# When transfers make the weight sums of the down projection: 18 from the output projection on, 14 during up

## The chip, the cores and the metric

The kernel runs on one core of a Trainium2 chip. A core has TensorE for matmuls (PE in the profile; PEld is its loading of weights), VectorE (DVE), ScalarE (ACT), GpSimd (POOL) and SyncE (SP), which only issues transfers. Transfers run on 16 DMA engines that the queues of SP, ACT and POOL share. The metric is the device time of one execution in microseconds, taken as the median over several runs.

## The reference

One encoder block on 512 tokens of width 2048, all in float32: a mixer of gated-DeltaNet and RWKV-7 heads, a cross-attention into 256 memory tokens, and an MLP, each added to the residual stream.

```python
xn = _rmsnorm(h, norm_mix[l])
y = xn @ w_in[l]
mixed = jnp.concatenate([o_gdn, o_rwkv], axis=-1)     # from y, the two mixers
h = h + mixed @ w_out[l]                              # the output projection
h = h + _cross_attention(...)
hn = _rmsnorm(h, norm_mlp[l])
h = h + jnp.square(jax.nn.relu(hn @ mlp_w_up[l])) @ mlp_w_down[l]   # up, then down; hidden 8192
return _rmsnorm(h, norm_final)
```

## The kernel before

Every float32 matmul is made of three: both operands are split into a high part (a cast, on ACT, L130) and a low part (a subtraction, on DVE, L131), and high x high, high x low and low x high are added up in PSUM. So every weight tile of 128x1024 passes through a load by SP, a cast whi on ACT and a subtraction wlo on DVE before TensorE gets it.

Up and down use a scheme with seven products in place of eight (Strassen in Winograd's form). In up this works on groups: `strassen(p, ...)` for p = 0 to 31 makes 256 of the 8192 hidden columns from four weight blocks (`a11`, `a21`, `a22`, `a12`, loaded at L1432) and sums of them made by DVE (L1408). The seven products go to PSUM tiles x, y and z. ACT and DVE bring them to two tiles of SBUF, c1 and c2, which come from a pool of three buffers, tag `sl`. The group ends with a square of c1 and of c2 on ACT (L1548), and the results, with two differences that DVE makes (t and t4), are written to DRAM (`Cd`, cd in the profile) by four transfers from ACT's queue:

```python
nc.scalar.dma_start(Cd[p // 2][:, 2:4, h], v(c2))     # L1497
nc.scalar.dma_start(Cd[p // 2][:, 0:2, h], v(c1))     # L1498
nc.scalar.dma_start(Cd[p // 2][:, 4:6, h], v(t))      # L1499
nc.scalar.dma_start(Cd[p // 2][:, 6, h], t4)          # L1500
```

The next group begins, for ACT, with the copy of x to the next c1 (L1466), and then with that of y to the next c2 (L1472), whose buffer is the one that L1497 is read from. A scheduler puts the instructions of each engine in order and adds the waits; an instruction behind a waiting one on the same engine waits too.

Down reads the hidden values back and takes four quarters (c = 0 to 3) of the hidden dimension one after another. Two of its seven products need sums of weight blocks. There are 32 of them, 1 MB each: `SUMS[0][u]` and `SUMS[1][u]` for u = 0 to 15, tiles in DRAM named ws in the profile, of which u = 4c to 4c + 3 belong to quarter c, the four of `SUMS[0]` needed ahead of the four of `SUMS[1]`. No engine computes these sums: POOL issues one transfer that copies a block from `w_dn` to the tile (L1304, shape 16x16384), waits until it has landed, and issues a second that adds the other block to it on the way (L1305, 512x512). `background` does this for all 32 in a row, held in that order. It is called in the output projection once the first of its 16 row blocks is there; a POOL copy of one column (L1301) makes it wait for that block. The two transfers of one sum are in order; the next sum's copy is issued right behind the add.

Of the kernel before, what the change touches and what calls it, by code (L numbers as in the profile page):

```python
# [9 lines left out]
F32 = mybir.dt.float32  # L10
F32R = mybir.dt.float32r
AF = mybir.ActivationFunctionType
ALU = mybir.AluOpType
# [4 lines left out]
P = 128  # L18
# [55 lines left out]
def build(tc, I, out):  # L74
    nc = tc.nc
    V, S, GP, PE = nc.vector, nc.scalar, nc.gpsimd, nc.tensor
    es = ExitStack()

    pc = es.enter_context(tc.tile_pool(name="pc", bufs=1))
# [18 lines left out]
    def col(name, i=0):  # L98
        o, w = PRM[name]
        return prm[:, o + i:o + i + 1]  # L100
# [17 lines left out]
    def psb(nm, tag="mx", bufs=2):  # L118
        return tile_of(ps, [P, 512], F32, tag, nm, bufs)
# [8 lines left out]
    def split(src, hi, lo, gain=None):  # L128
        if gain is None:
            S.copy(hi, src)  # L130
            V.tensor_tensor(out=lo, in0=src, in1=hi.bitcast(F32), op=ALU.subtract)  # L131
        else:
            S.activation(hi, src, AF.Copy, scale=gain)
            V.scalar_tensor_tensor(out=lo, in0=src, scalar=gain, in1=hi.bitcast(F32),
                                   op0=ALU.mult, op1=ALU.subtract)
# [20 lines left out]
    def gemm(pt, wsrc, nk, hi, lo):  # L156
        for h in range(nk // 8):
            wh, wl = wload(wsrc[:, h * 1024:(h + 1) * 1024] if nk > 8 else wsrc)
            for kk in range(8):
                k = h * 8 + kk  # L160
                sl = slice(kk * P, (kk + 1) * P)
                mm(pt, wh[:, sl], hi[k], start=(k == 0), stop=False)
                mm(pt, wh[:, sl], lo[k], start=False, stop=False)
                mm(pt, wl[:, sl], hi[k], start=False, stop=(k == nk - 1))
# [172 lines left out]
    def act_tile(nm, dt=F32R):  # L337
        return tile_of(pa, [P, 512], dt, "act", nm, 32)
# [5 lines left out]
    SUMS = {i: [pd.tile([P, 2048], F32, name=f"ws{i}_{u}", tag=f"ws{i}_{u}") for u in range(16)] for i in (0, 1)}  # L344
# [884 lines left out]
    hres = [hq[n // 4][n % 2][:, n // 2 % 2, :] for n in range(16)]  # L1229
# [4 lines left out]
    def sl2(w=512):  # L1234
        cnt[0] += 1
        return ph.tile([P, 512], F32, tag="sl", name=f"sl{cnt[0]}", bufs=3)[:, 0:w]
# [18 lines left out]
    for n2 in range(8):  # L1255
        hi, lo = act_tile(f"vhi{n2}"), act_tile(f"vlo{n2}")
        for i in range(2):
            n = 2 * n2 + i
# [11 lines left out]
            u, t = rstd[:, M:2 * M], sl2(M)  # L1270
# [7 lines left out]
    for g in range(4):  # L1278
        for h in range(4):
            pts = [psb(f"vo{g}_{h}_{mt}", ("mm", "mg")[h % 2]) for mt in range(2)]  # L1280
            for q in range(2):
                wh, wl = wload(I["wo"][g, h][:, q * 1024:(q + 1) * 1024])
                for mt in range(2):
                    for e in range(2):
                        d = q * 2 + e
# [9 lines left out]
                nc.scalar.dma_start(VOd[g][:, h * 2 + mt, :], ev)  # L1295


    def background(h):

        d = pc.tile([P, 1], F32, name="began")  # L1300
        tc.keep_in_program_order(GP.tensor_copy(d, h[:, 0:1]))  # L1301
        for u in range(16):
            for i, b in ((0, 2), (1, 0)):
                tc.keep_in_program_order(GP.dma_start(SUMS[i][u], I["w_dn"][u, b]))  # L1304
                tc.keep_in_program_order(GP.dma_start(SUMS[i][u], I["w_dn"][u, 1], accum_op=ALU.add, max_dma_last_dim=2048))  # L1305

    def finish(n, acc):
        if n == 0:
            S.activation(acc, hres[n], AF.Square)
        else:  # L1310
            sq = sl2()
            S.activation(sq, hres[n], AF.Square)
            V.tensor_tensor(out=acc, in0=acc, in1=sq, op=ALU.add)
# [3 lines left out]
    for n in range(KD):  # L1317
        xr = sl2()
        nc.sync.dma_start(xr, I["xT"][:, n, :])
        pt = psb(f"op{n}", "mm", 2)  # L1320
        gemm(pt, I["w_out"][n], KD, oh, ol)
        V.tensor_tensor(out=hres[n], in0=pt, in1=xr, op=ALU.add)
        hi, lo = act_tile(f"hh{n}"), act_tile(f"hl{n}")
        split(hres[n], hi, lo, col("norm_xattn", n))
        hh_.append(hi)
        hl_.append(lo)
        finish(n, acc)
        if n == 0:
            background(hres[n])
    pcol = psb("pcol")  # L1330
    for t in range(4):
        mm(pcol[:, t:t + 1], acc[:, t * P:(t + 1) * P], ones[:, 0:1])
# [10 lines left out]
    for g in range(2):  # L1343
        pts = [psb(f"sc{g}_{t}", ("mm", "mm", "mg", "mg")[t]) for t in range(4)]
        for n2 in range(8):
# [7 lines left out]
            for i in range(2):  # L1353
                n = 2 * n2 + i
# [49 lines left out]
    def sub(o, a, b):  # L1404
        V.tensor_tensor(out=o, in0=a, in1=b, op=ALU.subtract)

    def add(o, a, b):
        V.tensor_tensor(out=o, in0=a, in1=b, op=ALU.add)  # L1408
# [17 lines left out]
    def raw(src, own=None):  # L1426
        i = nraw[0] % 7 if own is None else own
        nraw[0] += 1
        r = pw.tile([P, 1024], F32, tag="wraw", name=f"ua{nraw[0]}", bufs=NWR) if i % 2 else \
            pu.tile([P, 1024], F32, tag="wraw2", name=f"ub{nraw[0]}", bufs=4)  # L1430
        if src is not None:
            nc.sync.dma_start(r, src)  # L1432
        return r

    def block(pt, a, parts, start):
        cnt[0] += 1
        hi = pw.tile([P, 1024], F32R, tag="whi", name=f"whi{cnt[0]}", bufs=NWS)
        lo = pw.tile([P, 1024], F32R, tag="wlo", name=f"wlo{cnt[0]}", bufs=NWS)
        split(a, hi, lo)
        for k in range(8):  # L1440
            for x in parts[k]:
                PE.matmul(pt, hi[:, k * P:k * P + P], x, start=start, stop=False, skip_group_check=True)  # L1442
                start = False
        for k in range(8):
            PE.matmul(pt, lo[:, k * P:k * P + P], parts[k][0], start=False, stop=k == 7, skip_group_check=True)  # L1445

    def strassen(p, done, used):

        def product(i, pt, a, start=True):
            block(pt[:, HA], a, [(comb[i][k][:, HA], comb[i][k][:, HB]) for k in range(8)], start)
            if used:
                used(i)

        if p == 0:
            a11, a12, a22, a21 = (raw(I["w_up"][p, i], o) for i, o in ((0, 1), (3, 1), (2, 1), (1, 0)))
        else:
            a11, a21, a22, a12 = (raw(I["w_up"][p, i]) for i in range(4))  # L1460
        s1 = raw(None, 0 if p == 0 else None)
        x, y, z = (psb(f"up{n}{p}", t) for n, t in (("x", "mx"), ("y", "mg"), ("z", "mm")))
        c1, c2 = sl2(), sl2()

        product(B11, x, a11)
        S.copy(c1[:, HA], x[:, HA])  # L1466
        if p == 0:
            product(B21, z, a12)
            sub(c1[:, HA], c1[:, HA], z[:, HA])
        add(s1, a21, a22)  # L1470
        product(T1, y, s1)
        S.copy(c2[:, HB], y[:, HA])  # L1472
        add(s1, s1, a11)
        product(T2, x, s1, False)
        S.copy(c1[:, HB], x[:, HA])
        add(a21, a21, a11)
        if p > 0:
            product(B21, z, a12)
            sub(c1[:, HA], c1[:, HA], z[:, HA])
        add(a12, a12, s1)  # L1480
        product(T3, x, a21, False)
        add(c2[:, HB], c2[:, HB], x[:, HA])
        product(B22, y, a12, False)
        add(c1[:, HB], c1[:, HB], y[:, HA])
        done(c1, ALU.min)
        product(T4, x, a22, False)
        S.copy(c2[:, HA], x[:, HA])
        done(c2, ALU.max)
        t = pu.tile([P, T], F32, tag="tt", name=f"tt{p}", bufs=2)
        t4 = pu.tile([P, M], F32, tag="t4", name=f"t4_{p}", bufs=1)  # L1490
        sub(t[:, HA], c1[:, HB], c1[:, HA])
        sub(c1[:, HB], c1[:, HB], c2[:, HB])
        sub(t[:, HB], c1[:, HA], c1[:, HB])
        sub(t4, c2[:, HA], t[:, HB])
        h = slice(p % 2 * M, p % 2 * M + M)
        v = lambda a: a.rearrange("p (a b) -> p a b", b=M)
        nc.scalar.dma_start(Cd[p // 2][:, 2:4, h], v(c2))  # L1497
# [3 lines that stand above are left out]
# [44 lines left out]
    for p in range(32):  # L1545
        def square(c, op):
            V.scalar_tensor_tensor(out=c, in0=c, scalar=0.0, in1=rstd, op0=op, op1=ALU.mult)
            S.activation(c, c, AF.Square)  # L1548

        def used(i):  # L1550
            if p == 0 and i == T1:
                pt = psb("pss2", "scr", 1)
                mm(pt, ones, acc)
                rsq(rstd, pt, 1.0 / 2048, b_eps6)
            if p == 31 and i in (T1, T2, T3):
                for q in ((0,), (1, 2), (3,))[i - T1]:
                    piece_(0, 0, q)

        strassen(p, square, used)
# [224 lines left out]
```

## Time and profile before

| | |
|---|---|
| median of three runs | 3033.95 us |
| lowest and highest | 3027.75, 3034.09 us |
| the profiled execution | 3031.7 us, its span 3029.9 us |
| TensorE busy | 2977.6 us (98%), granted clock 0.995 on average |
| ACT, DVE, POOL busy | 1481.0, 2078.6, 266.2 us |
| POOL's transfers (queue q0) | 67.11 MB, 9.2% of the 16 DMA engines' span |
| output projection | from 1333 us on |
| up | about 1690 to 2343 us |

In the profile's rows, "out<-in" names what an instruction writes and reads, "[6.55 <-DMA cd<-sl]" is idle time of its engine just before it and what ended that. Times in order of time are microseconds from the span's start, then the duration. ACTq and SPq are transfers that these engines' queues issue.

### The profile page before, as it was taken

To read this page: it belongs to the slowest core of one execution; us is meant where nothing else is said; L and a number is where in the kernel's file an instruction comes from. 1 tells how busy PE (TensorE), PEld (TensorE's weight loads), DVE (VectorE), ACT (ScalarE), POOL (GpSimd) and SP (SyncE) were. 2 spreads that over 40 slices of the span, in tenths; PEclk is the share of its full clock that TensorE was granted. 3 is DMA by queue.
4 is the path that set the end of the run, shared out by engine and by line. 5 is a ranking of instruction groups with operands and counts; after the bars stand their busy time and mean duration, and the time that the engine had idled before them with its cause. 6 is when DMAs were issued, how large, how long until landed. Compare 5 with 4: busy or idle time off the path is not lost.

```text
span 3029.9 us, 56109 instructions
## 1 busy us (share of the span) xinstructions
PE 2977.6 (98%) x22912; PEld 2677.1 (88%) x22912; DVE 2078.6 (69%) x2925; ACT 1481.0 (49%) x2000; POOL 266.2 (9%) x612
## 2 busy tenths in 40 slices
PE   9999999999999999999999889999999999999998
PEld 7788878878877898878887889999999999999998
DVE  7666666676677646534337778888888786868676
ACT  6454555554556555543326544444444544444444
POOL 0302312213213000001111100000000000000000
PEclk9999999999999999999999999999999999999999
DMA  5322323322425487789999974544544877676754
GB/s 185 102 87 80 108 79 83 108 81 81 136 65 164 149 269 239 253 266 265 260 252 261 247 228 154 153 149 146 161 147 147 278 243 239 213 250 197 241 181 153
DMA packets 284625, 537.70 MB, mean 177 GB/s; under 512 B 95752, under 2 KB 148236, under 8 KB 283856
## 3 DMA queue, kind: packets, MB, share of 16 engines
q1 hardware_dynamic: 228816, 427.15, 45.6%
q0 software_dynamic: 17920, 67.11, 9.2%
q10 hardware_dynamic: 37632, 39.86, 3.8%
q8 instruction: 179, 2.93, 0.4%
q14 instruction: 78, 0.64, 0.1%
HBM read 473.86 MB, written 127.28 MB: 198 GB/s over the span
## 4 chain that ended last, share of the span: by engine, by line
PE 89%; DMA 4%; DVE 3%; ACT 2%; issue 1%; POOL 0%; SPq 0%; DVEq 0%; ACTq 0%; POOLq 0%
PE py L247 21%; PE upx L1442 7%; PE dx L1442 7%; PE op L122 6%; PE upy L1442 4%; PE upx L1445 4%; PE dx L1445 4%; PE dy L1442 3%; PE vo L122 3%; PE sc L122 3%; PE at L122 3%; PE vp L122 3%; PE kq L247 3%; PE kp L247 3%; PE upz L1442 2%; PE upy L1445 2%
## 5 line engine op out<-in xcount | busy, mean ns | idle before, releaser
L130 ACT CAST whi<-ub 128x1024 fp32r<-128x1024 f32 x259 | 271.0, 1048 | 288.3 <-PE dx L1442 69.8
L131 DVE TENSOR_TENSOR wlo<-ub,whi 128x1024 fp32r<-128x1024 f32 x259 | 316.1, 1222 | 98.0 <-ACT whi L130 97.8
L247 PE MATMUL py<-xhi,whi 128*128 128x512 f32 x928 | 371.6, 400 | 6.6 <-ACT xhi L247 6.6
L247 PE MATMUL py<-xhi,wlo 128*128 128x512 f32 x928 | 372.0, 401 | 0.0
L247 PE MATMUL py<-xlo,whi 128*128 128x512 f32 x928 | 371.3, 400 | 0.0
L247 DVE TENSOR_TENSOR wlo<-wraw,whi 128x1024 fp32r<-128x1024 f32 (+1 forms) x180 | 223.4, 1241 | 128.7 <-ACT whi L247 127.0
L130 ACT CAST whi<-ua 128x1024 fp32r<-128x1024 f32 x189 | 198.0, 1048 | 212.2 <-PE dx L1442 51.8
L247 ACT CAST whi<-wraw 128x1024 fp32r<-128x1024 f32 (+1 forms) x180 | 188.2, 1045 | 204.1 <-PE py L247 161.9
L1442 PE MATMUL upx<-cb,whi 128*128 128x256 f32 x2048 | 268.5, 284 | 4.3 <-ACT whi L130 4.3
L131 DVE TENSOR_TENSOR wlo<-ua,whi 128x1024 fp32r<-128x1024 f32 x189 | 230.6, 1221 | 60.7 <-ACT whi L130 58.6
L1442 PEld LDWEIGHTS upx<-cb,whi 128*128 128x128 f32 x2048 | 256.5, 193 | 4.9 <-ACT whi L130 4.7
L1442 PE MATMUL dx<-dh,whi 128*128 128x256 f32 x1024 | 252.0, 284 | 3.1 <-ACT whi L130 3.1
L1442 PE MATMUL dx<-dl,whi 128*128 128x256 f32 x1024 | 251.2, 283 | 0.0
L131 DVE TENSOR_TENSOR wlo<-wraw,whi 128x1024 fp32r<-128x1024 f32 x112 | 137.3, 1226 | 111.3 <-ACT whi L130 109.9
L247 PEld LDWEIGHTS py<-xhi,whi 128*128 128x128 f32 x928 | 175.0, 189 | 40.9 <-ACT xhi L247 6.6
L247 PEld LDWEIGHTS py<-xhi,wlo 128*128 128x128 f32 x928 | 175.0, 189 | 35.3 <-issue 1.0
L247 PEld LDWEIGHTS py<-xlo,whi 128*128 128x128 f32 x928 | 174.9, 188 | 35.1 <-DVE xlo L247 0.7
L1442 PEld LDWEIGHTS dx<-dh,whi 128*128 128x128 f32 x1024 | 196.5, 192 | 4.3 <-ACT whi L130 4.1
L1442 PEld LDWEIGHTS dx<-dl,whi 128*128 128x128 f32 x1024 | 196.5, 192 | 0.0
L130 ACT CAST whi<-wraw 128x1024 fp32r<-128x1024 f32 x112 | 117.8, 1051 | 151.7 <-PE op L122 68.9
L1445 PE MATMUL upx<-cb,wlo 128*128 128x256 f32 x1024 | 144.5, 284 | 0.0
L1445 PE MATMUL dx<-dh,wlo 128*128 128x256 f32 x1024 | 143.8, 283 | 0.1
(782 smaller groups left out, 6982.5 us busy)
## 6 DMA issues: line engine op xcount, KB each, us to landing
wraw<-in_w_in SPq DMA_DIRECT2D x116, 512.0 KB, 3.8
ub<-in_w_dn SPq DMA_DIRECT2D x88, 512.0 KB, 5.1
ua<-in_w_dn SPq DMA_DIRECT2D x72, 512.0 KB, 4.9
ub<-in_w_up SPq DMA_DIRECT2D x71, 512.0 KB, 4.4
ws<-in_w_dn POOLq DMA_DIRECT2D x32, 1024.0 KB, 10.8
ua<-in_w_up SPq DMA_DIRECT2D x57, 512.0 KB, 4.3
sl<-cd SPq DMA_DIRECT2D x104, 256.0 KB, 5.3
ub<-ws SPq DMA_DIRECT2D x40, 512.0 KB, 5.1
```

The costliest lines, as they stand in the source:

```text
L122: PE.matmul(o, l, r, start=start, stop=stop)
L130: S.copy(hi, src)
L131: V.tensor_tensor(out=lo, in0=src, in1=hi.bitcast(F32), op=ALU.subtract)
L247: f(*a, **k)
L1442: PE.matmul(pt, hi[:, k * P:k * P + P], x, start=start, stop=False, skip_group_check=True)
L1445: PE.matmul(pt, lo[:, k * P:k * P + P], parts[k][0], start=False, stop=k == 7, skip_group_check=True)
```

## The change

`background` gets a count. Its first call, at the same place, makes 18 sums. Each further call makes one: it stands in `strassen` behind odd groups from p = 3 on, as long as any sum is left, that is 14 times, the last at p = 29. There ACT copies one column of the finished c2 to a column of a small tile `ticks`, POOL copies that to `tock`, and so waits for it, and then issues the two transfers. The sums are made in the order in which down needs them: the four of `SUMS[0]` of a quarter, then the four of `SUMS[1]`. Lines behind the change move by 3 to 6.

```diff
-    def background(h):
-
-        d = pc.tile([P, 1], F32, name="began")
-        tc.keep_in_program_order(GP.tensor_copy(d, h[:, 0:1]))
-        for u in range(16):
-            for i, b in ((0, 2), (1, 0)):
-                tc.keep_in_program_order(GP.dma_start(SUMS[i][u], I["w_dn"][u, b]))
-                tc.keep_in_program_order(GP.dma_start(SUMS[i][u], I["w_dn"][u, 1], accum_op=ALU.add, max_dma_last_dim=2048))
+    ticks = pc.tile([P, 32], F32, name="ticks")
+    tock = pc.tile([P, 1], F32, name="tock")
+    wanted = [(i, c * 4 + u) for c in range(4) for i in (0, 1) for u in range(4)]
+
+    def background(h, n):
+
+        tc.keep_in_program_order(GP.tensor_copy(tock, h[:, 0:1]))
+        for _ in range(n):
+            i, u = wanted.pop(0)
+            tc.keep_in_program_order(GP.dma_start(SUMS[i][u], I["w_dn"][u, (2, 0)[i]]))
+            tc.keep_in_program_order(GP.dma_start(SUMS[i][u], I["w_dn"][u, 1], accum_op=ALU.add, max_dma_last_dim=2048))
...
         if n == 0:
-            background(hres[n])
+            background(hres[n], 18)
...
         sub(t4, c2[:, HA], t[:, HB])
+        if p % 2 and p > 1 and wanted:
+            S.copy(ticks[:, p:p + 1], c2[:, 0:1])
+            background(ticks[:, p:p + 1], 1)
         h = slice(p % 2 * M, p % 2 * M + M)
```

POOL around the 19th sum, before (ws is a sum's tile, in_w_dn the weights; 16x16384 is the copy, 512x512 the add):

```order
L1304 DMA ws_8_144<-in_w_dn 16x16384
L1305 DMA ws_8_144<-in_w_dn 512x512
L1304 DMA ws_9_129<-in_w_dn 16x16384
L1305 DMA ws_9_129<-in_w_dn 512x512
L1304 DMA ws_9_145<-in_w_dn 16x16384
L1305 DMA ws_9_145<-in_w_dn 512x512
```

And in the changed kernel:

```order
L1308 DMA ws_9_129<-in_w_dn 512x512
L1304 COPY tock<-ticks 128x1
L1307 DMA ws_10_130<-in_w_dn 16x16384
L1308 DMA ws_10_130<-in_w_dn 512x512
L1304 COPY tock<-ticks 128x1
L1307 DMA ws_11_131<-in_w_dn 16x16384
```

Ahead of each sum from the 19th on now stands a copy that waits for ACT's tick. ACT from the end of group p = 3 to the next group's second copy, before (sl are c1 and c2, upx and upy PSUM tiles, ua and ub weight blocks, tt and t the differences):

```order
L1548 ACTIVATE sl_17434<-sl_17434 128x512
L1497 DMA cd_153<-sl_17434 128x2x256
L1466 COPY sl_17668<-upx_17665 128x256
L130 CAST whi_17730<-ua_17664 128x1024
L1498 DMA cd_153<-sl_17433 128x2x256
L1499 DMA cd_153<-tt_17646 128x2x256
L1500 DMA cd_153<-t_3_17647 128x256
L1472 COPY sl_17669<-upy_17666 128x256
```

And in the changed kernel:

```order
L1554 ACTIVATE sl_17407<-sl_17407 128x512
L1499 COPY ticks<-sl_17407 128x1
L1503 DMA cd_153<-sl_17407 128x2x256
L1469 COPY sl_17645<-upx_17642 128x256
L130 CAST whi_17707<-ua_17641 128x1024
L1504 DMA cd_153<-sl_17406 128x2x256
```

The tick stands between the square of c2 and the transfer that writes c2; the rest of ACT's order is as it was.

## The prediction

> **What bounds the kernel now.** I read the page first, then a table of stretches, the waits, the instructions of two engines in order of time, and at the end the DMA queues in very short windows. The page's head and its first two parts:
>
> ```profile
> span 3029.9 us, 56109 instructions
> PE 2977.6 (98%) x22912; PEld 2677.1 (88%) x22912; DVE 2078.6 (69%) x2925; ACT 1481.0 (49%) x2000; POOL 266.2 (9%) x612
> PE   9999999999999999999999889999999999999998
> ```
>
> TensorE is the bound: it idles 52 us in all, and only two slices of 40, the 23rd and 24th (1667 to 1818 us), show less than nine tenths. That is where up begins, while POOL still makes weight sums. One group of up is the time from one L1466 copy to the next. A table of stretches cut there (stretch, its length, busy time of each engine, granted clock, DMA share, GB/s):
>
> ```profile
> core 0: us, PE busy (x) PEld busy (x) DVE busy (x) ACT busy (x) POOL busy (x), PEclk, DMA share, GB/s
> 1722.44:1748.00 25.56, 21.74 (x171) 21.53 (x170) 16.70 (x21) 9.59 (x14) 1.83 (x3) 0.93 0.99 270
> 1748.00:1769.25 21.25, 20.20 (x168) 19.98 (x167) 16.20 (x21) 9.68 (x14) 3.09 (x4) 1.00 0.92 271
> 1769.25:1798.51 29.26, 22.44 (x172) 22.23 (x171) 17.12 (x21) 9.58 (x13) 1.03 (x1) 0.88 0.81 211
> 1798.51:1818.67 20.16, 20.16 (x170) 20.16 (x170) 16.66 (x21) 9.66 (x14) 0.00 (x0) 1.00 0.54 164
> ...
> 1798.51:2342.60 544.09, 544.09 (x4536) 544.09 (x4536) 450.49 (x541) 262.08 (x352) 0.00 (x0) 1.00 0.49 151
> ```
>
> Three groups take 25.56, 21.25 and 29.26 us; the 27 after them take 544.09, 20.15 each, with TensorE busy for all of it. Against 20.16 the three lose 5.40, 1.09 and 9.10: 15.6 us. The waits of 1700 to 1800, and of 1800 to 2340 (last row), say on what:
>
> ```profile
> ACT sl L1472 <- DMA cd<-sl: 15.8, 2, 9.2
> ...
> ACT sl L1472 <- DMA cd<-tt: 3.8, 1, 3.8
> PE upz L1442 <- ACT whi L130: 11.7, 3, 6.8
> ```
> ```profile
> ACT sl L1472 <- DMA cd<-sl: 3.6, 2, 1.9
> ```
>
> ACT stands at L1472, the copy into the next group's c2, until the write of the old c2 to cd has landed; the weight casts stand behind it in ACT's order, and the product z waits for its cast. ACT in order of time, in the worst places and in an undisturbed group:
>
> ```profile
> 1722.02 0.38 ACTq L1497 DMA_DIRECT2D cd<-sl  x1
> 1722.44 0.37 ACT L1466 COPY sl<-upx 128x256 f32<-128x256 f32 x1 [0.45 <-PE upx L1445]
> ...
> 1730.43 0.37 ACT L1472 COPY sl<-upy 128x256 f32<-128x256 f32 x1 [6.55 <-DMA cd<-sl]
> ...
> 1753.18 0.37 ACT L1472 COPY sl<-upy 128x256 f32<-128x256 f32 x1 [3.78 <-DMA cd<-tt]
> ...
> 1817.54 0.63 ACT L1548 ACTIVATE sl<-sl 128x512 f32<-128x512 f32 x1 [1.10 <-DVE sl L1547]
> 1818.20 0.37 ACTq L1497 DMA_DIRECT2D cd<-sl  x1
> 1818.67 0.37 ACT L1466 COPY sl<-upx 128x256 f32<-128x256 f32 x1 [0.49 <-PE upx L1445]
> ...
> 1821.32 0.37 ACT L1472 COPY sl<-upy 128x256 f32<-128x256 f32 x1 [1.26 <-PE upy L1445]
> 1821.59 1.05 ACT L130 CAST whi<-ub 128x1024 fp32r<-128x1024 f32 x1
> ```
> ```profile
> 1824.16 1.92 PE upz L1442 x16
> ```
>
> The last row is from the chain that ended last. Undisturbed, L1472 starts 2.65 us after L1466 and is released by TensorE, not by the write. Its cast ends at 1822.64 and z starts at 1824.16: 1.52 us of slack, so L1472 may start as late as 1822.84 at no loss. The stretches check this: 1753.18 is 5.18 after its L1466, 2.53 late, 1.01 over the slack, and that group lost 1.09. The longer stalls lose more than the rule gives (3.8 for the first, 5.40 lost), and the granted clock of 0.93 and 0.88 in these groups shows the rest.
>
> **The change part by part.** Removed: all sums after the 18th before up. POOL in order of time, first, 18th and last sum (L1304 copies 1 MB, L1305 adds 1 MB):
>
> ```profile
> 1344.88 0.18 POOL L1301 COPY began<-h 128x1 f32<-128x1 f32 x1 [378.56 <-DVE h L1322]
> 1345.01 0.69 POOL L1304 DMA_DIRECT2D ws<-in_w_dn  x1
> 1350.55 1.06 POOL L1305 DMA_DIRECT2D ws<-in_w_dn  x1 [4.85 <-DMA ws<-in_w_dn]
> ...
> 1588.76 1.02 POOL L1305 DMA_DIRECT2D ws<-in_w_dn  x1 [12.01 <-DMA ws<-in_w_dn]
> ...
> 1781.80 1.03 POOL L1305 DMA_DIRECT2D ws<-in_w_dn  x1 [13.35 <-DMA ws<-in_w_dn]
> ```
>
> The 18th add is issued at 1588.76 and would be done some 15 us later, over 100 us before the first c2 write at 1722. So the first c2 writes of up meet weight loads alone, as from 1798 on, and the three groups should take 20.16 each: **gain 15.6 us**. More is not to be had, since the rest of up is full; it is 14.5 if the 1.09 is something else. In attention and the output projection nothing is gained: no wait of TensorE there ends with a transfer.
>
> Added: behind each odd group from the 4th on (p = 3, 5, ... 29), one ACT copy of 128x1, one POOL copy of 128x1, and one sum, 14 times. The price of the ACT copy is bounded by a like one (from the groups by line):
>
> ```profile
> L1677 ACT ACTIVATE rcol<-rstd 128x1 f32<-128x1 f32 x1 | 0.2, 202 | 0.0
> ```
>
> 0.2 us in front of L1466, whose followers have over 1 us of slack: nothing. If that cover is gone, 14 x 0.2 = 2.8 us. POOL serves nothing else, so its waits cost nothing by themselves.
>
> The sum's transfers are the price. The tick is issued between the Square and L1497, so the 1 MB copy starts in the same moment as the c2 write that L1472 needs. The queues in short windows, of the first sum's copy (1346.3 to 1346.5, then 1346.3 to 1349.9) and of one undisturbed c2 write (1818.2 to 1820.0), as packets, MB and share of 16 engines:
>
> ```profile
> q0 software_dynamic: 7, 0.46, 696.8%
> ```
> ```profile
> q0 software_dynamic: 32, 1.05, 81.4%
> ```
> ```profile
> q10 hardware_dynamic: 272, 0.26, 43.5%
> ```
>
> The copy is one 64 KB packet for each of 16 engines (7 packets are 0.46 MB), it starts about 1346.4, 1.5 us after POOL's L1301 began, and holds the engines until 1349.8, 3.4 us. The c2 write is all started before 1820.0, that is 1.8 us after its issue. Set the Square's end (1818.17) to 0: the tick ends near 0.25, POOL starts some 0.1 later, the copy's packets come at 1.85. The write, issued at 0.05 to 0.1, ends at 1.85 to 1.95. It is a tie. A write that escapes costs nothing (and nothing below that: TensorE is busy 544.09 of 544.09 us). A caught one ends behind the packet, at 5.25, L1472 starts near 5.35 and the latest harmless start is 4.67: 0.7 us. The nearest row, the group that lost 1.09 beside a running sum, gives the upper end. So 14 sums cost 0 to 15.3; I take six caught at 0.7, **4 us**, since the copy reaches 9 engines at once and the rest up to 0.8 later, when the write is over.
>
> The Trainium skill, DMA: Bandwidth & Descriptors, section Queues, rings and completion order, says that each DMA engine switches between queues only at packet boundaries. This speaks against the change: a 64 KB packet is never interrupted, and the trace agrees, 1 MB in 3.4 us. The same page's Specifications put the first byte of a transfer from gpsimd at about 1 us and from scalar at about 0.6; by that the copy would come before the write is over, all 14 would be caught, and by my price of 0.7 the cost would be 9.8 and not 4. The trace has 1.4 us from issue to the first packet.
>
> The same packet delays the weight load issued just then. Its rows in a later group (SP and DVE in order of time, the chain, and the page's median landing):
>
> ```profile
> 1839.20 0.33 SPq L1432 DMA_DIRECT2D ub<-in_w_up  x1
> ```
> ```profile
> 1846.98 1.22 DVE L1408 TENSOR_TENSOR ub<-ua,ub 128x1024 f32<-128x1024 f32 x1
> 1848.12 0.41 DVE L1405 TENSOR_TENSOR sl<-sl,upz 128x256 f32<-128x256 f32 x1
> 1848.45 1.22 DVE L131 TENSOR_TENSOR wlo<-ua,whi 128x1024 fp32r<-128x1024 f32 x1
> ```
> ```profile
> 1850.08 1.92 PE upy L1442 x16
> ```
> ```profile
> ub<-in_w_up SPq DMA_DIRECT2D x71, 512.0 KB, 4.4
> ```
>
> 4.4 + 3.4 after 1839.20 is 1847.0, when DVE wants it: nothing to 0.5 us late, and wlo behind it, over at 1849.67, is wanted only after upy's first 1.92 us, at 1852.0. Covered. In 8 groups the new order also puts the z subtraction ahead of that addition, which leaves the load more room. The add's packets come some 5 us after the copy's and meet loads that are issued 10 us and more ahead of use; the waits of 1700 to 1800, where sums ran nearly all the time, name no weight load. The order of use changes nothing: the last sum, started near 2320, is of down's fourth quarter.
>
> Sum: the profiled execution is 3031.7 us (span 3029.9 and 1.8 around it), 2.3 below the median of the three runs, 3033.95, and inside their range of 3027.75 to 3034.09. 3031.7 - 15.6 + 4 = **3020**.
>
> **The rivals.** *Every sum catches its c2 write* (22 in 100): for it, the tie above; against it, the late start of the copy on 7 engines. 14 x 0.7 to 14 x 1.09: 3026 to 3031, gain nearly spent. *The stalls get long enough to halve TensorE's clock* (7): the place is the same L1472; if the copy and the running add stand before the write together, each sum costs what the first stalled group did, 5.40, in all 76, and 3092. It is slower than before from 1.1 us a sum on, and by over 0.2% from 1.55. Against it: the add starts only after the copy has landed, some 5 us on. *The first groups stall anyhow* (5), because what held the c2 writes was not the sums: 3031.7. Against it: 27 groups with the same loads and no sums never lost a microsecond.
>
> **How the numbers follow.** My forecast (63 in 100) holds 3016 to 3024: none caught with the full gain, ten caught (7.0) with 14.5. The range adds the first rival above, to 3031, and 3 us below for the spread of the runs: 3013. The remaining 3 in 100 are things I don't see. About 0.2% (6 us) is what a measurement of this kernel can tell from no change. Faster by more: the forecast and a quarter of the first rival, 0.68. Within: the rest of it and the third, 0.23. Slower: 0.09.
>
> **What would show it.** POOL's 19th sum starts in up near 1785, and the 18th is over by 1605. The groups up to p = 3 take 20.16 us and the granted clock stays 1.00 after the first group. L1472's waits on DMA come behind odd groups alone; where one is longer than 1.52 us beyond the usual start, that group exceeds 20.16 by the difference. I am wrong if each odd group is followed by a loss of over a microsecond, or if the loss at up's start remains.

## The result, and the profile after

Over 14 runs each the changed kernel takes 3021.18 us in the median (3017.20 to 3029.51), the kernel before 3032.67 (3024.39 to 3038.09): a ratio of 0.9967, 95% interval 0.9958 to 0.9977. The forecast was 3020, in a range of 3013 to 3031. The profiled execution has a span of 3016.8 us where the one before had 3029.9, so 13.1 us are to be explained. (The two profiled executions lie 1.0 and 2.6 us below these medians, so the profiles show 1.6 us more gain than the medians do.) In the changed kernel the lines behind the change have moved: the copies L1466 and L1472 are now L1469 and L1475, the four writes to cd L1503 to L1506, the weight load L1435, the adds of weights L1411; the tick is L1499, POOL's copy into tock L1304, the 1 MB copy L1307 and the add L1308.

The page's head, as shown of before:

```profile
span 3016.8 us, 56151 instructions
PE 2972.4 (99%) x22912; PEld 2672.2 (89%) x22912; DVE 2077.9 (69%) x2925; ACT 1484.6 (49%) x2014; POOL 271.8 (9%) x626
PE   9999999999999999999999999999999999999998
```

The dent in the 23rd and 24th slice is gone. POOL in order of time, the 18th add and the 19th sum:

```profile
1593.30 1.02 POOL L1308 DMA_DIRECT2D ws<-in_w_dn  x1 [13.20 <-DMA ws<-in_w_dn]
1780.30 0.49 POOL L1304 COPY tock<-ticks 128x1 f32<-128x1 f32 x1 [185.97 <-ACT ticks L1499]
1780.73 0.51 POOL L1307 DMA_DIRECT2D ws<-in_w_dn  x1
```

The table of stretches, cut at groups of up (p = 1, 2, 3, then 6, 10, 24, and 25 to 29 together; columns as before the change):

```profile
core 0: us, PE busy (x) PEld busy (x) DVE busy (x) ACT busy (x) POOL busy (x), PEclk, DMA share, GB/s
...
1719.91:1740.12 20.21, 20.21 (x171) 20.21 (x170) 16.71 (x21) 9.70 (x14) 0.00 (x0) 1.00 0.49 150
1740.12:1760.05 19.93, 19.93 (x168) 19.93 (x168) 16.39 (x21) 9.77 (x14) 0.00 (x0) 1.00 0.57 169
1760.05:1780.72 20.67, 20.67 (x174) 20.67 (x173) 17.48 (x22) 9.87 (x14) 0.42 (x1) 1.00 0.46 145
1820.76:1841.59 20.83, 20.49 (x170) 20.26 (x169) 16.66 (x21) 9.66 (x14) 1.82 (x3) 1.00 0.90 246
1901.83:1924.86 23.03, 20.64 (x172) 20.44 (x171) 17.03 (x21) 9.59 (x13) 1.24 (x2) 1.00 0.82 221
2186.71:2208.78 22.07, 20.64 (x172) 20.44 (x171) 17.04 (x21) 9.60 (x14) 1.24 (x2) 1.00 0.82 230
2208.78:2309.69 100.91, 100.91 (x842) 100.86 (x841) 83.22 (x101) 48.77 (x69) 4.12 (x7) 1.00 0.68 192
```

The three groups that took 25.56, 21.25 and 29.26 us take 20.21, 19.93 and 20.67: 15.3 us come back there. Two groups now stand out, 23.03 and 22.07 us, those behind the sums of p = 9 and p = 23; group 6, behind that of p = 5, takes 20.83. TensorE is busy for 20.64 us in groups 10 and 24 and idle for the rest; the five groups of the last row, with two sums among them, take 20.18 each. I count the 30 groups p = 1 to 30 against 30 x 20.16 us and call the difference their excess: it was 15.4 us before and is 4.9 now. Group 10 brings 2.6 of it, group 24 1.7 (each less the 0.23 us that the group ahead of it is short), group 6 0.7, and the other groups cancel out to 0.1. Of the other 2.6 us that the span lost, 1.85 stand already at 1147 us, in code that both kernels share.

ScalarE in order of time behind p = 9, and behind p = 11, whose group lost nothing:

```profile
1900.78 0.19 ACT L1499 COPY ticks<-sl 128x1 f32<-128x1 f32 x1
1900.79 0.37 ACTq L1503 DMA_DIRECT2D cd<-sl  x1
...
1903.53 4.34 ACTq L1505 DMA_DIRECT2D cd<-tt  x1
...
1908.57 0.37 ACT L1475 COPY sl<-upy 128x256 f32<-128x256 f32 x1 [4.79 <-issue]
...
1944.56 0.19 ACT L1499 COPY ticks<-sl 128x1 f32<-128x1 f32 x1
1944.57 0.37 ACTq L1503 DMA_DIRECT2D cd<-sl  x1
...
1946.16 0.43 ACTq L1505 DMA_DIRECT2D cd<-tt  x1
1946.68 0.63 ACTq L1506 DMA_DIRECT2D cd<-t  x1
1947.72 0.37 ACT L1475 COPY sl<-upy 128x256 f32<-128x256 f32 x1 [1.30 <-DVE wlo L131]
```

What the reader is to see is the second column of the ACTq rows. Issuing a transfer takes ScalarE about 0.4 us. The issue of L1505 behind p = 9 takes 4.34 us (behind p = 23, 3.45 us), and L1475 starts once it and the short issue behind it are over. The bracket behind L1475 says "issue", and behind p = 23 it says "PE upx L1448": the view of waits counts an issue neither as work nor as a wait and puts its length down to whatever came before. POOL, SP and the transfer queues tell why, first p = 9, then p = 11 (the queues from 1902.7 to 1903.0, from 1945.3 to 1948.0, and from 1948.0 to 1948.4):

```profile
1901.10 0.18 POOL L1304 COPY tock<-ticks 128x1 f32<-128x1 f32 x1 [29.70 <-ACT ticks L1499]
...
1901.54 0.51 POOL L1307 DMA_DIRECT2D ws<-in_w_dn  x1 [0.25 <-issue]
...
1902.76 0.33 SPq L1435 DMA_DIRECT2D ua<-in_w_up  x1
```
```profile
q0 software_dynamic: 9, 0.59, 663.0%
```
```profile
1944.88 0.49 POOL L1304 COPY tock<-ticks 128x1 f32<-128x1 f32 x1 [35.54 <-ACT ticks L1499]
...
1945.32 0.51 POOL L1307 DMA_DIRECT2D ws<-in_w_dn  x1
...
1945.39 0.33 SPq L1435 DMA_DIRECT2D ub<-in_w_up  x1
```
```profile
q1 hardware_dynamic: 92, 0.38, 63.2%
```
```profile
q0 software_dynamic: 7, 0.46, 390.2%
q1 hardware_dynamic: 18, 0.07, 51.7%
```

Behind p = 9 the copy's 64 KB packets (queue q0) start at 1902.76, 1.22 us after their issue, and hold the engines until about 1907.7; ScalarE's third write is issued in that time and stands. Behind p = 11 SP issues a 512 KB weight load (q1) 0.07 us after the copy. Its first packets come first, no packet of the copy starts before 1948.0, 2.7 us after its issue, and by then all four writes have been issued. In both cases the write of c2 landed 2.07 us after its issue. Behind 12 of the 14 sums a weight load steps in front of the copy like this, and the longest issue there takes 1.51 us. Behind p = 9 and 23 none does: VectorE puts a weight subtraction (L131) in front there, so the addition behind which the load is issued, and the differences that the second to fourth write wait for, all come 1.15 us later than behind p = 11.

The load that steps in front is slowed by the copy in turn. The eleven of these loads whose landing the trace tells took 7.5 to 10.2 us from issue to landing, where a load of up took 4.4 in the median before. The longest, issued 0.08 us behind the copy of p = 5, kept VectorE waiting:

```profile
1831.36 1.23 DVE L1411 TENSOR_TENSOR ub<-ua,ub 128x1024 f32<-128x1024 f32 x1 [1.77 <-DMA ub<-in_w_up]
```

That is the group of 20.83 us, 0.67 over 20.16. So 11 of the 14 sums cost 0.1 us or less, two cost a stuck issue, and one a late weight load.

### The profile page after: what moved, and what is told of

It is laid out like the page before. It is cut to its first block, busy times and chain, and to the rows that moved or that the text cites. A ratio compares the mean times of both kernels' runs of the same rounds, so it can differ in the third digit from the quotient of the medians.

```text
span 3016.8 us, 56151 instructions
## 1 busy us (share of the span) xinstructions
PE 2972.4 (99%) x22912; PEld 2672.2 (89%) x22912; DVE 2077.9 (69%) x2925; ACT 1484.6 (49%) x2014; POOL 271.8 (9%) x626
## 4 chain that ended last, share of the span: by engine, by line
PE 92%; DMA 2%; DVE 2%; ACT 2%; issue 1%; POOL 0%; ACTq 0%; SPq 0%; DVEq 0%; POOLq 0%
PE py L247 21%; PE upx L1445 8%; PE dx L1445 7%; PE op L122 6%; PE dx L1448 4%; PE upy L1445 4%; PE upx L1448 4%; PE dy L1445 4%; PE kq L247 3%; PE vo L122 3%; PE vp L122 3%; PE sc L122 3%; PE at L122 3%; PE kp L247 2%; PE dz L1445 2%; PE upy L1448 2%
## 5 line engine op out<-in xcount | busy, mean ns | idle before, releaser
L131 DVE TENSOR_TENSOR wlo<-ub,whi 128x1024 fp32r<-128x1024 f32 x259 | 316.1, 1221 | 90.9 <-ACT whi L130 90.3
L131 DVE TENSOR_TENSOR wlo<-ua,whi 128x1024 fp32r<-128x1024 f32 x189 | 230.7, 1221 | 58.3 <-ACT whi L130 56.5
L131 DVE TENSOR_TENSOR wlo<-wraw,whi 128x1024 fp32r<-128x1024 f32 x112 | 137.2, 1225 | 114.3 <-ACT whi L130 112.8
L1448 PE MATMUL upx<-cb,wlo 128*128 128x256 f32 x1024 | 144.1, 283 | 0.0
L1448 PE MATMUL dx<-dh,wlo 128*128 128x256 f32 x1024 | 143.8, 283 | 0.1
```

## The experiments

Ratios are to the kernel before, run beside each. "Excess" is that of groups 1 to 30, as above.

**1. No sums in up.** The 14 ticks and sums of up are taken out. This kernel leaves these sums out altogether: down reads the one block where it needs the sum of two, by the same number of transfers.

```
-        if p % 2 and p > 1 and wanted:
-            S.copy(ticks[:, p:p + 1], c2[:, 0:1])
-            background(ticks[:, p:p + 1], 1)
...
-        src = SUMS[b - 4][u] if b >= 4 else I["w_dn"][u, b]
+        src = (I["w_dn"][u, (2, 0)[b - 4]] if (b - 4, u) in wanted else SUMS[b - 4][u]) if b >= 4 else I["w_dn"][u, b]
```

> Left out: the 14 sums of up; their blocks are read in down as they lie in memory, unsummed, so the same number of transfers reads them. It measures what the 14 sums cost in all. Theory (a sum costs only where its 1 MB copy reaches the DMA engines before ScalarE has issued the four writes to cd; ScalarE then stands in the issue of the third, L1505, until the copy is over; this happens behind p = 9 and p = 23 alone): the groups of up take 20.16 us each in the mean, the excess of groups 1 to 30 falls from 4.9 us to about 0, and the span from 3016.8 to about 3012, ratio to the kernel before about 0.995. Rival (each sum also costs something elsewhere, by the bandwidth it takes from the weight loads): a span of 3008 or less, the missing time outside up.

As the theory had it: ratio 0.9937 (0.9922 to 0.9952), span 3011.9 us, 4.9 below the changed kernel's. The table of stretches, groups 1 to 30 in one:

```profile
1719.11:2323.72 604.61, 604.61 (x5041) 604.61 (x5040) 500.96 (x601) 291.33 (x392) 0.00 (x0) 1.00 0.50 152
```

30 x 20.16 is 604.8: the excess is gone (-0.2 us), and TensorE never idles. The 14 sums cost 4.9 us of the span in all, and about 3012 is the floor for any placing of them in up.

**2. The sums of p = 9 and 23 moved to 14 and 28.**

```
-        if p % 2 and p > 1 and wanted:
+        if p in (3, 5, 7, 11, 13, 14, 15, 17, 19, 21, 25, 27, 28, 29):
```

> The 14 sums stay, but those behind p = 9 and p = 23 move to p = 14 and p = 28; nothing else changes. Theory (only these two places cost, since there the copy comes 1.5 us earlier): groups 10 and 24 fall from 23.03 and 22.06 us to the 20.39 they had before, groups 15 and 29 gain at most 0.3, span about 3012.5, ratio to the kernel before about 0.995. Rival (each sum costs alike, about 0.35 us, or two of any 14 are caught by chance): two other groups or all of them lose the same 4 to 5 us, span 3016 to 3018.

Half a miss. Groups 10 and 24 take 20.38 and 20.39 us, as expected. But group 15 takes 23.96 and group 28 24.92, the excess is 8.4 us and the span 3022.8; the ratio is 0.9958 (0.9942 to 0.9974), no better than the changed kernel's. The two new losses are the same stuck issue, of L1506 this time:

```profile
2002.57 0.52 POOL L1307 DMA_DIRECT2D ws<-in_w_dn  x1
...
2002.95 0.33 SPq L1435 DMA_DIRECT2D ua<-in_w_up  x1
...
2004.00 4.33 ACTq L1506 DMA_DIRECT2D cd<-t  x1
...
2271.07 4.09 ACTq L1506 DMA_DIRECT2D cd<-t  x1
```

Behind p = 14 the load follows the copy by 0.38 us and not by 0.08, and the copy's packets start 1.24 us after their issue. VectorE does the same operations at the same distances there as behind p = 11, so it is the load's place and not a busy VectorE that lets the copy through. Behind p = 27 the copy starts 3.36 us after L1503, nearly as in the changed kernel (3.40); but the issue of L1505 had taken 1.41 us before the copy was there, and L1506 came into it. In the changed kernel the last issue took 1.51 us at this place and the group lost 0.1: it was a near miss all along. The profiled execution took 3024.59 us and the median of its kernel is 3019.43; the difference is about the 4.75 us of group 28, so that loss seems to fall on some executions only. That is worked out from the times and was not seen.

**3. The tick ahead of the Square of c2.**

```
+        if p % 2 and p > 1 and wanted:
+            S.copy(ticks[:, p:p + 1], c2[:, 0:1])
+            background(ticks[:, p:p + 1], 1)
         done(c2, ALU.max)
```

> The tick of each sum is put ahead of the Square of c2 in ScalarE's order, about 1.6 us earlier against the four writes. Theory (issue of L1505 stuck behind the copy): now the copies of the 12 groups that lost nothing come before the third write is issued; each loses what p = 9 and 23 lost, 1.9 to 2.9 us, so 23 to 35 us more: span 3040 to 3052, slower than before by 0.3 to 0.7 per cent. Rival one (what was predicted, the c2 write caught behind the packet, 0.7 us each): 14 x 0.7, span about 3022. Rival two (the place of the tick does not matter, each sum costs 0.35 us): span 3016 to 3018.

Ratio 1.0084 (1.0064 to 1.0105), span 3061.2, excess 46.7 us. The load is now issued 1.8 us or more after the copy, all 14 copies start 1.21 to 1.23 us after their issue, and 14 groups lose. Behind p = 11, ScalarE, and group 12 in the table of stretches:

```profile
1955.94 0.37 ACTq L1503 DMA_DIRECT2D cd<-sl  x1
...
1957.08 3.12 ACTq L1504 DMA_DIRECT2D cd<-sl  x1
...
1962.48 0.37 ACT L1475 COPY sl<-upy 128x256 f32<-128x256 f32 x1 [4.69 <-DMA cd<-sl]
```
```profile
1956.40:1980.27 23.87, 21.89 (x170) 21.69 (x169) 16.75 (x21) 9.54 (x14) 1.02 (x1) 0.93 0.69 191
```

Here the copy precedes the write of c2 itself, which lands 6.47 us after its issue, and that wait outlasts the stuck issue, in this group and in 12 of the 13 others. So this run shows the predicted mechanism at work, at 3.7 us in this group (3.3 in the mean of the 14) and not 0.7: 1.98 us of idle time, and 1.73 more because TensorE's clock is granted at 0.93 in that group. It adds 41.8 us to the excess and so went beyond the theory's 23 to 35: the theory had counted on the stuck issue and on no fall of the clock, which makes up 19.5 of the 46.7 us (TensorE is busy for 624.3 us in groups 1 to 30, where 604.8 were enough).

**4. The tick behind the fourth write.**

```
         nc.scalar.dma_start(Cd[p // 2][:, 6, h], t4)
+        if p % 2 and p > 1 and wanted:
+            S.copy(ticks[:, p:p + 1], t4[:, 0:1])
+            background(ticks[:, p:p + 1], 1)
```

> The tick of each sum is put behind the issue of the fourth write to cd in ScalarE's order, about 2 us later. Theory: no issue of a write stands behind a copy any more, groups 10 and 24 lose nothing, excess of groups 1 to 30 below 1 us, span about 3012.5, ratio to the kernel before about 0.995, the best so far with all sums made. Rival (the later copy catches what comes next, the weight load that DVE wants or the next writes): other groups lose 0.5 us or more each, span 3017 or more.

As the theory had it: ratio 0.994 (0.9924 to 0.9957), median 3014.8, span 3013.3, with all sums made. The copies start 5.8 to 6.9 us after the issue of the write of c2 (L1500 in this kernel), and the excess is 0.1 us:

```profile
1719.97:2324.86 604.89, 604.85 (x5041) 604.64 (x5040) 500.13 (x601) 293.39 (x405) 24.30 (x42) 1.00 0.69 200
```

**5. The early tick with the copy in 4 KB packets.**

```
-GP.dma_start(SUMS[i][u], I["w_dn"][u, (2, 0)[i]])
+GP.dma_start(SUMS[i][u], I["w_dn"][u, (2, 0)[i]], max_dma_last_dim=4096)
```

> The early tick again (before the Square of c2; its own run lost 46.7 us in groups 1 to 30 against 20.16 each, span 3061.2), and the 1 MB copy is cut into packets of 4 KB, 256 of them, where it had 16 of 64 KB. Theory (what holds ScalarE's writes is the length of the single packet, which no other queue can get into): the write of c2 and the copy take turns, L1504's issue is held for a second at most instead of 3.1 us, the excess falls from 46.7 to 20 us or less, span 3035 or less. Rival (it is the megabyte that stands in front, whatever its packets): excess 40 to 50 us, span 3055 to 3065.

Between the two: span 3045.5, excess 34.5, ratio 1.0052 (1.0038 to 1.0066). Behind p = 11:

```profile
1954.95 0.37 ACTq L1504 DMA_DIRECT2D cd<-sl  x1
1955.41 0.68 ACTq L1505 DMA_DIRECT2D cd<-tt  x1
...
1960.03 0.37 ACT L1475 COPY sl<-upy 128x256 f32<-128x256 f32 x1 [4.35 <-DMA cd<-sl]
```

The issues no longer stand (0.37 and 0.68 us where one took 3.12): that part is the long packet's doing. But the write of c2 still lands 6.14 us after its issue where it took 6.47, because the megabyte is still in front of it or between its packets. Smaller packets cure the stuck issue and hardly the late write. Nor is the lower excess due to the issues: in groups 1 to 30 TensorE's idle time falls only from 27.2 to 24.1 us, and the other 9 us are its clock, granted at 0.99 in place of 0.97: 5 stretches of 3.41 us at half clock and not 11 (see the last section).

**6. All 32 in one row, in the new order.**

```
-            background(hres[n], 18)
+            background(hres[n], 32)
```

(and no ticks in up)

> All 32 sums start in one row at the output projection, as before the change, but in the new order of use; the ticks in up are gone. Theory (the order of use is worth nothing; the place is all): span 3029 to 3033, the three groups after the first of up lose 15 us again, ratio to the kernel before 0.998 to 1.002. Rival (part of the gain comes from the order): span under 3025.

As the theory had it: ratio 1.0004 (0.9992 to 1.0016), span 3030.4, excess 18.0. Groups 1 and 2 take 29.77 and 28.47 us, group 3 20.48. The order of use is worth nothing that these runs can tell.

**7. All 32 in one row, begun at vp.**

```
+            if n == 0:
+                background(t, 32)
             split(t, h2, l2)
```

(and the call at the output projection is gone)

> All 32 sums in one row, in the new order, but begun 100 us sooner, at the start of the vp projection near 1148 us, so that at 13.6 us each the last is over near 1590, before up. Theory (the stalls come only from sums that stand beside up's writes): groups 1 to 30 lose nothing, span about 3012 to 3014, ratio to the kernel before about 0.994, as good as no sums in up at all. Rival (the sums then slow the vp and vo stages, whose weight loads already take 0.74 to 0.81 of the transfer engines): up loses nothing but the stages from 1148 to 1345 us grow by 5 us or more, span 3017 or more.

The rival, at almost 20 times the least it was given: ratio 1.0264 (1.0249 to 1.028), span 3105.2. Up is as free as in the first experiment (excess -0.2), but the stages vp and vo grow by 93 us. The stretch of vp, and that of vo, here and then in the changed kernel:

```profile
1147.86:1293.07 145.21, 109.66 (x515) 89.24 (x513) 64.42 (x92) 50.38 (x78) 15.74 (x20) 0.87 0.94 272
1293.07:1425.18 132.11, 106.07 (x385) 77.11 (x383) 40.37 (x37) 50.35 (x66) 11.50 (x16) 0.92 1.02 313
```
```profile
1147.00:1240.00 93.00, 92.77 (x515) 78.19 (x514) 66.52 (x92) 51.63 (x78) 0.00 (x0) 1.00 0.72 231
1240.00:1331.00 91.00, 91.00 (x386) 70.79 (x385) 41.01 (x36) 51.42 (x66) 0.00 (x0) 1.00 0.85 272
```

These stages take 231 and 272 GB/s for themselves; a row of sums beside them leaves TensorE waiting for weights (60 us of waits for the casts and subtractions of weights in vp and vo, and a granted clock of 0.87 and 0.92).

**8. No tick: POOL reads c2.**

```
-            S.copy(ticks[:, p:p + 1], c2[:, 0:1])
-            background(ticks[:, p:p + 1], 1)
+            background(c2, 1)
```

> The changed kernel without ScalarE's tick: POOL's copy into tock reads c2 itself, so POOL issues the 1 MB copy about 0.2 us earlier; all else stays. Theory (12 of 14 copies are harmless only because the weight load that SP issues 0.08 us after them reaches the transfer engines first and they wait 1.6 us behind it): the load now comes about 0.3 us after the copy, as behind p = 14 of the second experiment (0.38), where the copy was first; most of the 12 copies start 1.2 us after their issue instead of 2.5 to 3.1, and their groups lose 2 to 5 us each: span 3030 to 3060. Rival (the later start is POOL's own, beside a busy VectorE; or the 0.2 us do not reach the copy's issue): copies start 2.5 us after issue as now, span 3014 to 3020.

The rival, in its second form. Span 3014.7, ratio 0.9955 (0.9941 to 0.9969); the 12 copies still start 2.4 to 2.9 us after their issue and the two of p = 9 and 23 still cost (excess 3.3). POOL, and VectorE beside it, behind p = 11:

```profile
1943.58 0.72 POOL L1304 COPY tock<-sl 128x1 f32<-128x1 f32 x1 [35.25 <-ACT sl L1553]
1944.23 0.52 POOL L1307 DMA_DIRECT2D ws<-in_w_dn  x1
```
```profile
1943.03 1.22 DVE L1411 TENSOR_TENSOR ua<-ua,ub 128x1024 f32<-128x1024 f32 x1
```

POOL's one-column copy begins 0.3 us sooner than with the tick and ends no sooner: it takes 0.72 us where it took 0.49, and 0.18 behind p = 9. In all 24 such cases of these two kernels it ends 0.04 us behind VectorE's L1411, which adds two tiles of SBUF. The weight load is issued right behind the same L1411 (1945.39 in the changed kernel, where L1411 ends at 1945.33). So load and copy are issued 0.08 us apart whatever the tick does, and the order in which they reach the engines does not change.

**9. The third and fourth write on SP.**

```
-        nc.scalar.dma_start(Cd[p // 2][:, 4:6, h], v(t))
-        nc.scalar.dma_start(Cd[p // 2][:, 6, h], t4)
+        nc.sync.dma_start(Cd[p // 2][:, 4:6, h], v(t))
+        nc.sync.dma_start(Cd[p // 2][:, 6, h], t4)
```

> The changed kernel, but the third and fourth write of each group (t and t4 to cd) are issued by SP and no longer by ScalarE; the ticks stay where they are. Theory (behind p = 9 and p = 23 ScalarE loses its time inside the issue of the third write, 4.34 and 3.45 us, while the write of c2 itself landed 2.07 us after its issue): ScalarE has only two writes left to issue and both are issued before the copy holds the engines, so groups 10 and 24 lose under 0.5 us and groups 1 to 30 under 1 us in all where the changed kernel lost 4.9. SP may stand in the issue instead; the next weight load is wanted some 8 us later, which hides 4 us. Span 3012 to 3014. Rival (what was predicted: L1475 waits for the c2 buffer behind the packet, whoever issues the other writes): groups 10 and 24 lose 1.6 to 2.9 us again, span 3016 to 3018.

As the theory had it. Ratio 0.9946 (0.9933 to 0.9959), median 3013.32, span 3011.3, excess -0.2: the floor, with all sums made. Behind p = 9 the copy comes 1.97 us after L1503 as before, and now SP stands in the issue while ScalarE goes on:

```profile
1902.45 3.50 SPq L1505 DMA_DIRECT2D cd<-tt  x1
```
```profile
1903.69 0.37 ACT L1475 COPY sl<-upy 128x256 f32<-128x256 f32 x1
```

Experiments 4 and 9 are the two versions that beat both kernels: the interval of 4 lies wholly below the changed kernel's, that of 9 all but its last ten-thousandth.

**10. 18 at the output projection, 14 in a row behind p = 3.**

```
-        if p % 2 and p > 1 and wanted:
+        if p == 3:
...
-            background(ticks[:, p:p + 1], 1)
+            background(ticks[:, p:p + 1], 14)
```

> 18 sums from the output projection on as in the changed kernel, but the other 14 in one row, started behind p = 3, with no ticks between them. It is the half of the change that spares the first groups without the half that spreads the sums. Theory (a row of sums meets the writes of every group it runs beside, as groups 1 to 3 did in the kernel before at 1 to 9 us each, 5.2 in the mean): 14 sums at 13.6 us run beside 9 or 10 groups, 40 to 60 us lost, span 3052 to 3075. Rival (only the first groups of up are sensitive): span 3012 to 3020.

As the theory had it, if in fewer groups: ratio 1.0103 (1.0085 to 1.0121), span 3059.6, excess 44.5. The eight groups beside the row, and those behind it:

```profile
1781.59:1987.31 205.72, 177.29 (x1344) 175.87 (x1343) 133.46 (x161) 76.57 (x105) 21.47 (x29) 0.90 0.95 262
1987.31:2370.12 382.81, 382.81 (x3192) 382.81 (x3192) 317.19 (x381) 184.83 (x248) 0.00 (x0) 1.00 0.49 151
```

205.72 is 44.4 over 8 x 20.16. The first of the eight, in which only the first copy falls, loses nothing; the seven others, 5 to 11, lose 4.4 to 8.6 us each. So it is not the first groups of up alone that a row of sums stalls.

## Why the prediction was right, step by step

**The gain.** Forecast 15.6 us from three groups; they gave back 15.3, and the tenth experiment shows the cause from the other side. That nothing else gains in attention and the output projection held: between 1147 us and the start of up the two executions drift by 0.2 us. That the order of use changes nothing held (experiment 6), and so did the ScalarE tick's price of nothing: the kernels with it and all sums harmless lie at the floor.

**The cost.** Forecast 4 us as six caught writes at 0.7 and nothing for weight loads; measured 4.9, of which group 10 brings 2.6, group 24 1.7 and group 6 0.7. The sum came out nearly right from terms that were not what happened, and so by luck. Two steps failed.

The first is "a caught one ends behind the packet, at 5.25", with six caught. No write of c2 was caught behind a copy. The latest of the 14, behind p = 27, landed 4.33 us after its issue, when none of the copy's packets had ended, so something else held it; L1475 started 3.96 us after L1469, inside the 2.65 + 1.52 that the prediction allows. The groups that paid lost their time elsewhere: behind p = 9 and 23 the write of c2 had landed after 2.07 us, and what was caught is the issue of the third write, with all that stands behind it in ScalarE's order; experiment 9 shows it, since moving that issue to another engine takes the loss away with the copies where they were. I had priced the wait of a write and not the time an engine can spend in issuing one, though the row of L1497 in the prediction carries that column. The predicted mechanism exists (experiment 3), and its term was mis-sized too: 3.7 us in the group shown and not 0.7. There the copy's packets start 0.2 us after the write's issue, ahead of the whole write, which lands 2.3 us after the last of them, where I had let it end with them; and TensorE's clock falls.

The second is the start of the copy and what the load does to it. "The same packet delays the weight load issued just then" came true, near the 4.4 + 3.4 = 7.8 us of the forecast (7.5 to 10.2), and "covered" held in all but one group: the load of 10.2 us cost 0.67. What I had not seen is that the load delays the packet as well. My start of the copy, 1.85 us behind the Square, was that of a copy alone, and p = 9 and 23 show it: 1.97 after L1503. Behind the 12 others the load's first packets go first and move the copy to 3.3 to 3.8. What I called a tie was decided, in 12 places of 14, by a transfer that I had treated as the victim alone.

**The rivals.** "Every sum catches" was given 14 x 0.7 to 14 x 1.09. Experiment 3 is that rival, and it costs 46.7 us: outside my range, on the slower side. A tick 1.6 us earlier would have made the change a loss, so the range was too narrow on that side for what I knew. The rule that a row slower than 1.1 us a sum makes the kernel slower fits it: 3.3 us a sum, ratio 1.0084. The rival of a halved clock came with it: in experiment 3, 11 of the 14 losses bring a stretch at half clock, in the changed kernel none. That the first groups stall anyhow did not happen.

**Packets and first bytes.** With 64 KB packets an issue stood 3.12 us, with 4 KB packets it took 0.37, and the write of c2 landed after 6.47 and 6.14. The rule of the Trainium skill, DMA: Bandwidth & Descriptors, Queues, rings and completion order, that an engine changes queue only at packet boundaries, fits the first pair, if an issue stands because it needs an engine that is inside a packet, which no run took apart; it alone does not tell why the write lands as late behind 4 KB packets. A copy's first packet came 1.22 us after its issue, a load's about 1.0, and the load issued 0.08 us later went first. By the figures of the same page's Specifications I had all 14 writes caught and 9.8 us lost; the trace differs, with no write caught.

**What to look for.** The 19th sum near 1785 (1780.73), the 18th over by 1605 (its last packet ends at 1602.2), the first groups at 20.16 (20.21, 19.93, 20.67) and the granted clock at 1.00 came true. "L1472's waits on DMA come behind odd groups alone" was the wrong view to watch: the two losses stand there as "issue" and as a wait for TensorE.

Left open: which groups have their load at another place follows from the rotation of the seven weight tiles over two pools, by reading the code and from p = 2, 9, 16, 23, 30 looking alike; no run moved the load alone.

## What to carry to other kernels

A transfer that an in-order engine issues can hold that engine for microseconds when a long packet stands in front, and the view of waits does not call it a wait: read the duration column of the issue rows. Put the start of background transfers behind the last issue of the group, not ahead of it, or issue the writes from an engine that nothing waits for; either took the excess of groups 1 to 30 from 4.9 us to 0.1 or less. When transfers are started by the same event, their order is decided by tenths of a microsecond, so a harmless overlap in a trace should be moved on purpose in both directions before it is relied on.

## What the runs showed of the hardware

POOL's 128x1 copy takes 0.18 us at best. When it begins beside a VectorE addition or subtraction of two SBUF tiles it ends 0.04 us behind that, and took up to 0.72 us beside an addition and 0.81 beside a subtraction (experiment 3, behind p = 9 and 23). The Trainium skill, GPSIMD Engine Reference, Specifications, says that POOL's SBUF interfaces are shared with VectorE and contended by instructions with two SBUF inputs; the trace agrees.

In up a copy issued by POOL has its first packet 1.2 to 1.3 us after the start of its issue when the nearest load is issued 0.38 us or more behind it (the changed kernel and experiments 2, 3 and 8), where the prediction read 1.4 from the first copy of all; SP's load has it 1.0 to 1.1 us after its own when it comes 0.08 us behind a copy.

Which issue stands is not a matter of count: it was the third, the fourth and the second. Behind p = 9 the copy's 16 packets start from 1902.76 to 1903.26: L1504, issued at 1903.07, still passes, L1505 at 1903.53 stands. Behind p = 14 in experiment 2 they start from 2003.82 on and L1506 at 2004.00 stands; behind p = 11 in experiment 3 they start by 1957.04 and L1504 at 1957.08 stands. Time alone does not settle it either, since an issue 0.31 us behind the first packet passed in the first case and one 0.18 us behind it stood in the second. An issue can also take 0.9 to 1.9 us with no copy near, as L1500 at 1900.97 in the kernel before did with 1.72, and most of these stand beside a 16 KB packet of the queue of instructions (q8, there from 1900.94). ScalarE's issue seems to need the engines that the packets hold; no run took that apart.

An idle time of 2.4 us in group 10 of the changed kernel left the granted clock at 1.00, one of 1.98 in group 12 of experiment 3 brought 0.93 and 1.7 us of slower work. The length of a stall alone does not tell whether the clock falls; where it lies does. In up the clock is lowered in pieces of 3.41 us at half clock, and the pieces of one trace start whole multiples of 3.41 us apart. The one in group 12 of experiment 3 and the piece ahead of it:

```profile
1961.39:1964.80 3.41, 1.44 (x13) 1.23 (x12) 0.97 (x1) 2.31 (x4) 0.45 (x1) 1.00 1.02 273
1964.80:1968.21 3.41, 3.41 (x19) 3.41 (x18) 2.53 (x3) 0.99 (x2) 0.00 (x0) 0.50 1.09 180
```

The whole stall, 1.97 us, lies in the first piece. In the changed kernel the stall of group 10 lies across an edge at 1908.50, 0.95 us ahead of it and 1.44 behind it by the same view. Cut into such pieces, groups 1 to 30 of the twelve traces have 28 pieces at full clock with 1.78 us of idle time or more, and each is followed by a piece at half clock; of 14 with 1.0 to 1.70 us, none is. So a stall of two to three microseconds costs 1.7 us more or not by where it falls, and group 10 of the changed kernel had luck in the execution shown.
